# A two-layer decoder step on one Trainium2 core: the second half's first norm in steps of one feature tile, and GpSimd in written order inside the other norms

## The chip, the core and the metric

The kernel runs on one core of a Trainium2 chip. TensorE (PE in the profile) does the matmuls, VectorE (DVE), ScalarE (ACT) and GpSimd (POOL) do the elementwise work, and SyncE (SP) issues most of the transfers. The metric is the device time of one execution in microseconds (us). Lower is better.

## The reference, cut to what matters

One inference step through two layers: layer 0 mixes tokens with stick-breaking attention (16 heads of 64), layer 1 with an RWKV-7 recurrence. After each mixer comes a squared-ReLU MLP of width 4096. There are 1024 prompt tokens and 64 sample tokens (8 sequences of 8), and the model width D is 1024. Ahead of each of the four sub-layers stands an RMS norm whose shift and scale come from a conditioning vector, one vector for the prompt and one for each sample sequence:

```
def rmsnorm(x, g):
    x32 = x.astype(jnp.float32)
    y = x32 * lax.rsqrt(jnp.mean(x32 * x32, axis=-1, keepdims=True) + NORM_EPS)
    return (y * g.astype(jnp.float32)).astype(x.dtype)

def ada_norm(x, c, g, w_ada, b_ada):
    mod = jax.nn.silu(c) @ w_ada + b_ada
    shift, scale, gate = jnp.split(mod[:, None, :], 3, axis=-1)
    return rmsnorm(x, g) * (1 + scale) + shift, gate
```

The norm of sub-layer 0 feeds the q, k and v projections, those of sub-layers 1 and 3 feed the two MLPs, and that of sub-layer 2 feeds the RWKV projections.

## The kernel before, in words

**Layout and halves.** Activations lie with features on the 128 partitions and tokens along the free dimension, so x is eight feature tiles (NT = 8). The 1088 tokens are cut into two halves. Half A is columns 0 to 575, all prompt. Half B is columns 576 to 1087: 448 prompt columns and the 64 sample columns. The program goes A, then B, through each sub-layer.

**Matmuls.** Each float32 operand is split into a high part and a low part. `dense` (line 346) makes one output tile from 8 feature tiles with three matmuls for each (lines 356 to 358: high by high, low by high, high by low), into a PSUM tile `dq`. Three `dq` buffers exist. For half A one output tile takes two column groups of 288, so 48 matmuls; for half B one group of 512, so 24. A weight tile is loaded by SP (`wst`, line 339), rounded by ACT (`wh`, line 342) and its rest taken by DVE (`wl`, line 343), three buffers deep. `dn` is the copy of a finished projection tile out of PSUM, done by ACT or DVE in turn; SP then stores it.

**A norm.** `rms` (line 258) squares each feature tile on ACT (`sq`, line 265), sums over the partitions with four small matmuls for each tile (`ssq`, line 267), takes the root on ACT (`rv`, line 271), refines it with six small DVE instructions (lines 272 to 277), and spreads the result over the partitions with four matmuls (`rb`, line 281), whose copies form R. `norm_tiles` (line 313) then makes, for each feature tile, `hf` = x times R times scale, the high part `hhi` and the low part `hlo`. The prompt columns take one DVE instruction for `hf` (line 291), one on ACT for `hhi` (line 323) and one on DVE for `hlo` (line 324). The sample columns, which only half B has, take three GpSimd instructions for `hf` (lines 295 to 297), an ACT cast (line 132, reached through `split`), and one GpSimd instruction for `hlo` (line 304). `norm_split` runs `norm_tiles` through all eight tiles; it is called for sub-layers 1 and 3, for A and for B. Only the two calls for B give work to GpSimd.

**What sets the order.** Instructions are handed to a scheduling layer, which orders each engine's queue by itself: it goes through a timeline of its own and takes what is ready there, with the order of the code as priority. Each engine then runs its queue strictly in that order. Background work is a Python generator: `behind(work, rate)` registers it, and each triple of matmuls in `dense` calls `step`, which owes `rate` steps for 512 columns; one step runs the generator to its next `yield`. `beside` is a second such line.

**The start.** The norm of half A runs first. Then the projections of half A (24 output tiles) run with `second` behind them at one step for five 512-column triples. `second` is the first norm of half B. It reads x twice through `Passing` (line 102), each time in eight loads of 128 x 512 into the shared pool `n` (6 buffers), which the `dn` copies and `sq` use too. Before the change its first step is the whole of `rms`, then come eight steps of one tile each. Then the projections of half B run with attention, and later the RWKV units and chains, behind them.

Of the kernel before, what the change touches and what calls it, by code (L numbers as in the profile page):

```python
# [106 lines left out]
class Kern:  # L107
# [149 lines left out]

    def rms(self, x, pt, tmp, ps, tag, slot, rslot=None):

        nc = self.nc  # L260
        W, w = pt.W, pt.W // 4
        q = ps.tile([128, 512], F32, tag=tag, name="ssq")
        for f in range(NT):
            sq = tmp.tile([128, W], F32, tag=slot, name="sq")
            nc.scalar.activation(sq, x[f], AF.Square)
            for g in range(4):
                nc.tensor.matmul(q[32 * g:32 * g + 32, :w], self.ones32, sq[:, w * g:w * g + w],
                                 start=f == 0, stop=f == NT - 1)
        v = tmp.tile([128, 4, w], F32, tag=slot, name="rv")
        ms, r, t, y = (v[:, i, :] for i in range(4))  # L270
        nc.scalar.activation(r, q[:, :w], AF.Sqrt, bias=self.eps, scale=1.0 / D)
        nc.vector.tensor_scalar(ms, q[:, :w], 1.0 / D, EPS, ALU.mult, ALU.add)
        nc.vector.reciprocal(y, r)
        nc.vector.tensor_mul(t, y, y)
        nc.vector.tensor_mul(t, t, ms)
        nc.vector.tensor_scalar(t, t, -0.5, 1.5, ALU.mult, ALU.add)
        nc.vector.tensor_mul(r, y, t)
        R = tmp.tile([128, W], F32, tag=rslot or slot, name="R", bufs=2 if rslot else None)
        for g in range(4):
            qb = ps.tile([128, 512], F32, tag=tag, name="rb")  # L280
            nc.tensor.matmul(qb[:, :w], self.cst[:, C_SELB + 128 * g:C_SELB + 128 * g + 128], r,
                             start=True, stop=True)
            self.copy(R[:, w * g:w * g + w], qb[:, :w])
        return R

    def modulate(self, s, f, x, R, pt, t):

# [18 lines left out]
    def norm_split(self, s, x, R, pt, pool, tmp, slot):  # L306

        parts = ([], [])
        for _ in self.norm_tiles(s, x, R, pt, pool, tmp, slot, parts):
            pass  # L310
        return parts

    def norm_tiles(self, s, x, R, pt, pool, tmp, slot, parts):
# [32 lines left out]
    def dense(self, w, mts, hi, lo, pt, ps, evac):  # L346

        nc = self.nc
        kt = len(hi)
        for m in mts:  # L350
            wh, wl = self.weight(w[m])
            for c0, n in pt.ch:
                q = ps.tile([128, 512], F32, tag="dps", name="dq")[:, :n]
                for k in range(kt):
                    h, l = hi[k][:, c0:c0 + n], lo[k][:, c0:c0 + n]
                    nc.tensor.matmul(q, wh[:, k, :], h, start=k == 0, stop=False)  # L356
                    nc.tensor.matmul(q, wh[:, k, :], l, start=False, stop=False)  # L357
                    nc.tensor.matmul(q, wl[:, k, :], h, start=False, stop=k == kt - 1)  # L358
                    self.step(n)
                evac(m, c0, n, q)  # L360
# [1203 lines left out]
    def rest(self, ctx, lp, hp, xp, tmp, PS):  # L1564
        nc, I = self.nc, self.I
        A, B = HALF
        rms = lambda x, pt: self.rms(x, pt, tmp, PS, "dps", "n", "R")
        dense = lambda w, parts, pt, evac: self.dense(w, range(NT), *parts, pt, PS, evac)
        norm = lambda s, x, R, pt: self.norm_split(s, x, R, pt, hp, tmp, "n")
        self.ready = set()  # L1570

        def aside(*works, n=AS):
            with ExitStack() as ctx:
                ps = self.psum(ctx, (("aux", n),))
                for w in works:
                    yield from w(ps)

        def second(ps):

            self.RB = self.rms(Passing(self, I["x"], B, tmp), B, tmp, ps, "aux", "n", "R")  # L1580
            yield
            self.hB = ([], [])
            yield from self.norm_tiles(0, Passing(self, I["x"], B, tmp), self.RB, B, hp, tmp, "n",
                                       self.hB)


        self.load_c(tmp)
        self.load_params()
        self.load_x(A, xp)
        x = self.x  # L1590
        R = rms(x, A)
        for _ in aside(lambda ps: self.ada_steps(0, ps, "aux", (0, 4, 1, 5, 2, 6, 3, 7)), n=BG):
            pass
        self.att_setup(self.misc)
        self.xscr = self.dram.tile([NT, 128, T], F32, name="xscr")
        h = norm(0, x, R, A)
        self.behind(aside(second), 1 / 5)
        self.qkv(*h, A, tmp, PS)
        self.until(lambda: False)
        h = self.hB  # L1600
        self.behind(self.background(), RATE)
        self.beside(itertools.chain(self.ada_steps(0, PS, "aux", range(8, 12)),
                                    *(self.ada_steps(s, PS, "aux") for s in (1, 2, 3))), 40 / 180)
        self.qkv(*h, B, tmp, PS)
        self.beside(iter(()), 0.0)
        self.until(lambda: ("o", 0) in self.ready)
        self.beside(self.ahead(("o", 0), self.s_o, I["x"], A, hp, tmp), 1)
        self.beside(iter(()), 0.0)

        x, o = self.next  # L1610
        dense(I["sb_w_o"], o, A, self.residual(0, x, A, tmp))
        self.show("x1", x, A)
        R = rms(x, A)
        self.rw_setup(lp)
        self.ffn(1, x, *norm(1, x, R, A), A, hp, tmp, PS)
        self.show("x2", x, A)
        self.spill(x, A)
        self.until(lambda: ("o", 1) in self.ready)
        self.rw_late(ctx.enter_context(self.pool(name="lq", bufs=1)))
        self.ready.add("rw")  # L1620
        R = rms(x, A)
        r = self.rw_norm(x, R, A, hp, tmp)
        self.mixer_in(0, r, hp, tmp, PS, self.ahead(("o", 1), self.s_o, I["x"], B, hp, tmp))
        self.beside(iter(()), 0.0)
        x, o = self.next
        dense(I["sb_w_o"], o, B, self.residual(0, x, B, tmp))
        RB = rms(x, B)
        self.ffn(1, x, *norm(1, x, RB, B), B, hp, tmp, PS)
        self.show("x2", x, B)
        self.spill(x, B)  # L1630
        R = rms(x, B)
        r = self.rw_norm(x, R, B, hp, tmp)
        self.rw_shift()
        self.mixer_in(1, r, hp, tmp, PS, self.ahead(("y", 0), self.s_y, self.xscr, A, hp, tmp))
        self.until(lambda: ("y", 0) in self.ready)
        self.beside(iter(()), 0.0)
        x, y = self.next
        dense(I["rw_w_o"], y, A, self.residual(2, x, A, tmp))
        self.show("x3", x, A)
        R = rms(x, A)  # L1640
        self.ffn(3, x, *norm(3, x, R, A), A, hp, tmp, PS)
        self.until(lambda: False)
        with ExitStack() as ctx:
            xp = ctx.enter_context(self.pool(name="x2", bufs=8))
            xB = self.load_tiles(self.xscr, B, xp)
            y = ([], [])
            for _ in self.load_split(self.s_y, B, hp, tmp, y):
                pass
            dense(I["rw_w_o"], y, B, self.residual(2, xB, B, tmp))
            self.show("x3", xB, B)  # L1650
            R = rms(xB, B)
            self.behind(self.final(x, A, tmp, PS))
            self.ffn(3, xB, *norm(3, xB, R, B), B, hp, tmp, PS)
            self.until(lambda: False)
            for _ in self.final(xB, B, tmp, PS):
                pass
# [121 lines left out]
```

## Time and profile before

| | us |
|---|---|
| median of 3 runs | 3692.9 |
| lowest and highest run | 3689.04, 3694.14 |
| the profiled execution | 3692.01 |
| its span, first to last instruction | 3690.0 |
| PE busy in it | 3490.4 (95%) |
| DVE, ACT, POOL busy | 2326.5, 1604.9, 660.7 |

Rows of the timeline give start (us from the span's start), duration, engine, line, operation, output<-inputs, shapes, the count of merged instructions, and in brackets the engine's idle time before them with what ended it. Rows of the waits give the engine and operation that waited, what it waited for, total us, number of waits, longest. Rows of the windows give a stretch, its length, then each engine's busy us with its count of instructions, the granted TensorE clock as a share of full speed, the share of the DMA engines and the GB/s.

### The profile page before, as it was taken

To read this page: it belongs to the slowest core of one execution; us is meant where nothing else is said; L and a number is where in the kernel's file an instruction comes from. 1 tells how busy PE (TensorE), PEld (TensorE's weight loads), DVE (VectorE), ACT (ScalarE), POOL (GpSimd) and SP (SyncE) were. 2 spreads that over 40 slices of the span, in tenths; PEclk is the share of its full clock that TensorE was granted. 3 is DMA by queue.
4 is the path that set the end of the run, shared out by engine and by line. 5 is a ranking of instruction groups with operands and counts; after the bars stand their busy time and mean duration, and the time that the engine had idled before them with its cause. 6 is when DMAs were issued, how large, how long until landed. Compare 5 with 4: busy or idle time off the path is not lost.

```text
span 3690.0 us, 71087 instructions
## 1 busy us (share of the span) xinstructions
PE 3490.4 (95%) x26360; PEld 2777.1 (75%) x26360; DVE 2326.5 (63%) x4718; ACT 1604.9 (43%) x3342; POOL 660.7 (18%) x1180
## 2 busy tenths in 40 slices
PE   7999999899999999998899997989899999989998
PEld 5986667778888876876677775657788888868886
DVE  5366778785554556787846556557875666645444
ACT  4245566663333345634334445544433444432332
POOL 1023333320000001122212113021100111131111
PEclk8999999999999999999899997999899999999999
DMA  6466653319887785666344445556354444333232
GB/s 245 138 220 202 208 187 122 87 46 335 342 297 262 276 314 176 215 212 197 111 136 137 134 128 171 195 161 219 120 146 124 139 141 122 119 108 117 92 94 83
DMA packets 433003, 634.45 MB, mean 172 GB/s; under 512 B 144337, under 2 KB 244562, under 8 KB 432658
## 3 DMA queue, kind: packets, MB, share of 16 engines
q1 hardware_dynamic: 369394, 532.90, 44.6%
q10 hardware_dynamic: 63264, 97.02, 7.8%
q8 instruction: 209, 3.42, 0.4%
q14 instruction: 136, 1.11, 0.1%
HBM read 523.76 MB, written 106.01 MB: 171 GB/s over the span
## 4 chain that ended last, share of the span: by engine, by line
PE 45%; DVE 4%; DMA 3%; issue 2%; SPq 1%; ACT 1%; POOL 1%; ACTq 0%; DVEq 0%; POOLq 0%
PE dq L356 12%; PE dq L357 12%; PE dq L358 12%; PE qc L1327 1%; PE qc L1317 1%; PE qc L1336 1%; PE s L1144 1%; SPq L1215 1%; PE yq L1484 0%; PE bonq L1476 0%; DMA st<-s_st 0%; PE invq L1286 0%; PE lq L1082 0%; PE ssq L1432 0%; PE qc L1340 0%
## 5 line engine op out<-in xcount | busy, mean ns | idle before, releaser
L342 ACT CAST wh<-wst 128x512 fp32r<-128x512 f32 (+1 forms) x512 | 425.0, 834 | 756.6 <-PE dq L357 637.8
L356 PE MATMUL dq<-hhi,wh 128*128 128x288 f32 (+1 forms) x2112 | 710.2, 337 | 16.9 <-ACT hhi L132 16.1
L357 PE MATMUL dq<-hlo,wh 128*128 128x288 f32 (+1 forms) x2112 | 704.6, 334 | 5.0 <-DVE hlo L324 4.1
L358 PE MATMUL dq<-hhi,wl 128*128 128x288 f32 (+1 forms) x2112 | 703.6, 333 | 0.0
L343 DVE TENSOR_TENSOR wl<-wst,wh 128x512 fp32r<-128x512 f32 (+1 forms) x512 | 501.0, 979 | 274.5 <-ACT wh L342 245.5
L356 PE MATMUL dq<-uh,wh 128*128 128x288 f32 (+1 forms) x1536 | 509.6, 336 | 12.6 <-DVE x L371 5.9
L357 PE MATMUL dq<-ul,wh 128*128 128x288 f32 (+1 forms) x1536 | 508.0, 331 | 0.0
L358 PE MATMUL dq<-uh,wl 128*128 128x288 f32 (+1 forms) x1536 | 506.2, 332 | 1.9 <-DVE wl L343 1.9
L356 PEld LDWEIGHTS dq<-hhi,wh 128*128 128x128 f32 x2112 | 400.8, 190 | 67.3 <-issue 19.9
L357 PEld LDWEIGHTS dq<-hlo,wh 128*128 128x128 f32 x2112 | 400.6, 190 | 43.5 <-issue 7.3
L358 PEld LDWEIGHTS dq<-hhi,wl 128*128 128x128 f32 x2112 | 400.5, 190 | 41.9 <-issue 11.8
L371 DVE SCALAR_TENSOR_TENSOR x<-dq,mod,x 128x288 f32<-128x288 f32 (+1 forms) x432 | 245.9, 570 | 251.9 <-PE dq L358 249.6
L356 PEld LDWEIGHTS dq<-uh,wh 128*128 128x128 f32 x1536 | 289.1, 189 | 61.9 <-issue 15.0
L546 DVE TENSOR_TENSOR_SCAN prod<-prod 128x256 f32<-128x256 f32 (+5 forms) x264 | 242.1, 919 | 118.7 <-ACT prod L537 86.1
L358 PEld LDWEIGHTS dq<-uh,wl 128*128 128x128 f32 x1536 | 289.2, 189 | 32.2 <-issue 6.6
L357 PEld LDWEIGHTS dq<-ul,wh 128*128 128x128 f32 x1536 | 289.3, 189 | 27.0 <-issue 5.3
L377 POOL TENSOR_TENSOR x<-x,rs 128x64 f32<-128x64 f32 x144 | 118.4, 822 | 631.1 <-DVE rs L374 603.6
L356 PE MATMUL dq<-xhi,wh 128*128 128x288 f32 (+1 forms) x576 | 206.2, 358 | 4.4 <-ACT sg L974 2.1
L357 PE MATMUL dq<-xlo,wh 128*128 128x288 f32 (+1 forms) x576 | 199.4, 346 | 2.2 <-DVE xlo L304 1.8
L358 PE MATMUL dq<-xhi,wl 128*128 128x288 f32 (+1 forms) x576 | 197.9, 344 | 0.0
L547 DVE TENSOR_TENSOR beta<-beta,prod 128x256 f32<-128x256 f32 (+5 forms) x264 | 140.6, 536 | 29.0 <-POOL beta L592 8.8
L470 ACT CAST uh<-ut 128x288 fp32r<-128x288 f32 (+1 forms) x192 | 94.9, 495 | 127.5 <-DVE ut L468 127.1
(300 smaller groups left out, 6110.0 us busy)
## 6 DMA issues: line engine op xcount, KB each, us to landing
pagek<-cache_kT SPq DMA_DIRECT2D x128, 512.0 KB
pagev<-cache_v SPq DMA_DIRECT2D x128, 512.0 KB
adaw<-ada_w SPq DMA_DIRECT2D x192, 256.0 KB
wst<-w_up SPq DMA_DIRECT2D x96, 512.0 KB
wst<-w_down SPq DMA_DIRECT2D x192, 256.0 KB
st<-s_st SPq DMA_DIRECT2D x40, 672.0 KB
wst<-sb_w_qkv SPq DMA_DIRECT2D x48, 512.0 KB
wst<-w_up ACTq DMA_DIRECT2D x32, 512.0 KB
```

The lines of the kernel that those rows point to most:

```text
L342: nc.scalar.copy(wh, st)
L343: nc.vector.tensor_sub(wl, st, wh.bitcast(F32))
L356: nc.tensor.matmul(q, wh[:, k, :], h, start=k == 0, stop=False)
L357: nc.tensor.matmul(q, wh[:, k, :], l, start=False, stop=False)
L358: nc.tensor.matmul(q, wl[:, k, :], h, start=False, stop=k == kt - 1)
L371: nc.vector.scalar_tensor_tensor(xs, q[:, :np_], g, xs, ALU.mult, ALU.add)
L377: nc.gpsimd.tensor_add(xv, xv, t)
L470: nc.scalar.copy(a, t[:, :n])
L546: nc.vector.tensor_tensor_scan(r, r, r, 1.0 if carry is None else carry, ALU.mult, ALU.bypass)
L547: nc.vector.tensor_mul(beta[:, :w], beta[:, :w], p[:, 1:w + 1])
L1144: nc.tensor.matmul(qs[hd][:, 128 * x:128 * x + 128], BK[rows, u + x, 64 * hd:64 * hd + 128], AR[rows, :, c], start=True, stop=True)
L1215: nc.sync.dma_start(self.s_tt[m, r:r + 32, cs, 32 * blk:32 * blk + 32] .rearrange("s c t -> c s t"), lt[p:p + n])
```

## The change

`rms` becomes the generator `rms_steps`, which yields after each feature tile's square and sums and once at the end with R. Every caller but `second` still runs it through at once. `second` now goes through it step by step, so that its norm takes 17 background steps where it took 9. In `norm_split`, the loop over the tiles stands in a block in which GpSimd's instructions keep their written order: the scheduling layer may not move them against each other. The other engines are ordered as before, and `second`, which calls `norm_tiles` itself, is outside that block.

```
     def rms(self, x, pt, tmp, ps, tag, slot, rslot=None):

+        for R in self.rms_steps(x, pt, tmp, ps, tag, slot, rslot):
+            pass
+        return R
+
+    def rms_steps(self, x, pt, tmp, ps, tag, slot, rslot=None):
...
             for g in range(4):
                 nc.tensor.matmul(q[32 * g:32 * g + 32, :w], self.ones32, sq[:, w * g:w * g + w],
                                  start=f == 0, stop=f == NT - 1)
+            yield
...
-        return R
+        yield R
...
     def norm_split(self, s, x, R, pt, pool, tmp, slot):

         parts = ([], [])
-        for _ in self.norm_tiles(s, x, R, pt, pool, tmp, slot, parts):
-            pass
+        with self.tc.manual_schedule(engines={mybir.EngineType.Pool}):
+            for _ in self.norm_tiles(s, x, R, pt, pool, tmp, slot, parts):
+                pass
         return parts
...
-            self.RB = self.rms(Passing(self, I["x"], B, tmp), B, tmp, ps, "aux", "n", "R")
-            yield
+            for self.RB in self.rms_steps(Passing(self, I["x"], B, tmp), B, tmp, ps, "aux", "n", "R"):
+                yield
```

Lines of the changed kernel are 7 or 8 higher than those named above.

**PE in the second half's first norm.** `ssq` sums one square tile `sq`, `rb` spreads the root, and `dq` rows are the projections of half A. Before:

```order
L358 MATMUL dq_679<-hhi_433,wl_676 128x288
L267 MATMUL ssq_477<-sq_494,ones32_62 32x128 x4
L267 MATMUL ssq_477<-sq_502,ones32_62 32x128 x4
L267 MATMUL ssq_477<-sq_510,ones32_62 32x128 x4
L267 MATMUL ssq_477<-sq_518,ones32_62 32x128 x4
L267 MATMUL ssq_477<-sq_526,ones32_62 32x128 x4
L267 MATMUL ssq_477<-sq_534,ones32_62 32x128 x4
L281 MATMUL rb_551<-rv_542,cst_60 128x128
```

Now, at the third and fourth square:

```order
L365 MATMUL dq_629<-hlo_418,wh_591 128x288
L273 MATMUL ssq_480<-sq_563,ones32_62 32x128 x4
L366 MATMUL dq_629<-hhi_417,wl_592 128x288
L364 MATMUL dq_629<-hhi_423,wh_591 128x288
L365 MATMUL dq_629<-hlo_424,wh_591 128x288
L366 MATMUL dq_629<-hhi_423,wl_592 128x288
L364 MATMUL dq_629<-hhi_429,wh_591 128x288
L273 MATMUL ssq_480<-sq_608,ones32_62 32x128 x4
```

The last six sums stood in a row with `rb` right behind them. Now projection matmuls stand ahead of each of the six, 31, 5, 20, 12, 38 and 10 of them, and 47 more stand between the last sum and `rb`. The loads of x on SP's queue are spread among the stores of `dn` in the same way.

**GpSimd in the norm of sub-layer 3, half B.** Lines 295 to 297 make `hf`, line 304 makes `hlo`; the count at a row's end is of feature tiles. Before:

```order
L295 TENSOR_TENSOR hf<-x,R 128x64 x6
L296 TENSOR_TENSOR hf<-hf,mod_5465 128x64 x6
L297 TENSOR_TENSOR hf<-hf,mod_5465 128x64 x6
L304 TENSOR_TENSOR hlo<-hf,hhi 128x64 x4
L295 TENSOR_TENSOR hf<-x,R 128x64 x2
L304 TENSOR_TENSOR hlo<-hf,hhi 128x64 x2
L296 TENSOR_TENSOR hf<-hf,mod_5465 128x64 x2
L297 TENSOR_TENSOR hf<-hf,mod_5465 128x64 x2
L304 TENSOR_TENSOR hlo<-hf,hhi 128x64 x2
```

Now, with the buffer numbers kept, so that each `hf` number is one feature tile:

```order
L302 TENSOR_TENSOR hf_38917<-x_38501,R_38902 128x64
L303 TENSOR_TENSOR hf_38917<-hf_38917,mod3_5468 128x64
L304 TENSOR_TENSOR hf_38917<-hf_38917,mod3_5468 128x64
L311 TENSOR_TENSOR hlo_38923<-hf_38917,hhi_38922 128x64
L302 TENSOR_TENSOR hf_38928<-x_38503,R_38902 128x64
L303 TENSOR_TENSOR hf_38928<-hf_38928,mod3_5468 128x64
L304 TENSOR_TENSOR hf_38928<-hf_38928,mod3_5468 128x64
L311 TENSOR_TENSOR hlo_38934<-hf_38928,hhi_38933 128x64
```

Before, six tiles went through line 295, then six through 296, then six through 297, and the first `hlo` was the nineteenth instruction. Now it is the fourth, and each tile's `hlo` stands ahead of the next tile's first product. The norm of sub-layer 1, half B, shows the same two patterns.

**ACT in the norm of sub-layer 1, half B.** Here RWKV units of half A run in the background: `L`, `S` and `bkq` are theirs, `DMA s_st` and `s_l` are their stores, issued from ACT's queue. Before:

```order
L1161 COPY L<-s_20748 64x192
L271 ACT_TABLE_LOAD
L271 ACTIVATE rv<-ssq,eps 128x128
L1161 COPY L<-s_20770 64x192
L1161 COPY L<-s_20771 64x192
L1165 DMA s_st_9665<-S 64x576
L1161 COPY L<-s_20794 64x192
L1166 DMA s_st_9665<-S 128x576
L1176 COPY S<-bkq 128x320 x2
```

Now:

```order
L1173 DMA s_st_9668<-S 64x576
L1169 COPY L<-s_20801 64x192
L1173 DMA s_st_9668<-S 64x576
L1174 DMA s_st_9668<-S 128x576
L1184 COPY S<-bkq 128x320 x2
L1184 COPY S<-bkq 128x256 x2
L1189 DMA s_l<-L 128x576
L278 ACT_TABLE_LOAD
L278 ACTIVATE rv<-ssq,eps 128x128
```

The root `rv` stood ahead of most of a unit's copies. Now it stands behind all of them and behind the issue of the store `s_l`.

## The prediction

> **What bounds the kernel now.** I read the page first, then PE's waits, then windows and the timeline around the waits that the change touches.
>
> ```profile
> span 3690.0 us, 71087 instructions
> PE 3490.4 (95%) x26360; PEld 2777.1 (75%) x26360; DVE 2326.5 (63%) x4718; ACT 1604.9 (43%) x3342; POOL 660.7 (18%) x1180
> PE   7999999899999999998899997989899999989998
> ```
>
> PE is the bound: 95% busy, and at 80% or more in all slices but two. A stall of PE that goes is therefore time gained, unless a later stage gives it back. These waits of PE bear on the change:
>
> ```profile
> PE vq L140 <- ACT dn L132: 22.1, 4, 6.8
> PE ssq L267 <- ACT sq L265: 18.5, 10, 8.3
> PE dq L356 <- ACT hhi L132: 16.1, 2, 8.1
> PE rb L281 <- DVE rv L277: 16.0, 8, 3.8
> ```
>
> The third row is two waits of 8 us for the sample columns' cast. The windows show the three places (the second half's first norm; the norms of sub-layers 1 and 3 for half B) beside a steady stretch:
>
> ```profile
> 56.84:76.60 19.76, 10.35 (x77) 7.75 (x77) 7.17 (x15) 7.19 (x16) 5.64 (x11) 0.57 0.46 147
> 90.00:120.00 30.00, 30.00 (x229) 30.00 (x228) 10.25 (x13) 8.34 (x14) 3.11 (x5) 1.00 0.41 144
> 1776.87:1790.10 13.23, 5.45 (x12) 3.86 (x13) 10.62 (x19) 5.41 (x13) 13.15 (x28) 0.50 0.16 46
> 1790.10:1804.00 13.90, 13.90 (x62) 11.47 (x62) 11.89 (x30) 4.97 (x10) 1.81 (x6) 1.00 0.15 39
> 3298.40:3312.40 14.00, 5.46 (x12) 3.98 (x13) 10.17 (x15) 7.95 (x19) 13.74 (x31) 0.50 0.01 2
> ```
>
> At each place PE is idle for over 8 us and its granted clock drops to half. A steady 288-column matmul costs 30.00/229 = 0.131 us, a 512-column one 13.90/62 = 0.224 at full clock and 5.45/12 = 0.454 at half. GpSimd is busy nearly throughout the last two places.
>
> **Place 1, the second half's first norm.**
>
> ```profile
> 57.59 0.43 PE L267 MATMUL ssq<-sq,ones 128*32 128x128 f32 x8 [0.32 <-ACT sq L265]
> 57.72 7.93 SPq L102 DMA_DIRECT2D x<-x  x6
> 61.34 0.63 ACT L265 ACTIVATE sq<-x 128x512 f32<-128x512 f32 x1 [2.12 <-DMA x<-x]
> 62.02 0.65 PE L267 MATMUL ssq<-sq,ones 128*32 128x128 f32 x8 [4.01 <-ACT sq L265]
> 66.12 0.37 ACT L271 ACTIVATE rv<-ssq,eps 128x128 f32<-128x128 f32 x1 [0.82 <-PE ssq L267]
> 69.05 2.04 PE L281 MATMUL rb<-rv,cst 128*128 128x128 f32 x8 [3.05 <-DVE rv L277]
> 71.75 0.61 PE L356 MATMUL dq<-hhi,wh 128*128 128x288 f32 x1 [0.66 <-ACT dn L132]
> ```
>
> Six sums and the spread stand in a row in PE's queue, so PE waits for each load of x, then for the root, then for a copy that ACT could not do meanwhile. The window of 19.76 us holds 48 records of sums, 8 of the spread and 21 projections. At full clock they cost 6 x 0.43 + 1.0 (half of 2.04) + 21 x 0.131 = 6.4, so 13.4 is lost. Now 163 projections stand between these steps: 163 x 0.131 = 21 us for six loads and the root, 47 of them (6.2 us) ahead of the spread, where the root needs 2.9 (66.12 to 69.05). A load needed 3.6 us from issue to use (57.72 to 61.34), and 21/6 = 3.5 is there for each, with several under way. What moves with it: each x load now stands on SP between a store of `dn` and a weight load, and may hold that weight load until a buffer is free; three weight tiles, each good for 48 x 0.131 = 6.3 us, cover this. ACT squares between its `dn` copies and weight casts, and both reach PE sooner than before. The gaps of only 5, 10 and 12 projections are shorter than a load, so I keep 1.4 us of waits and count a gain of 12. Ends: 13.4 if no wait stays, 7 if three squares wait 2.12 as the one above. The eight tiles that follow keep their tile-by-tile order and lie beside projections, at no cost; if that cover were gone, they would cost what place 3 does.
>
> **Place 3, sub-layer 3, half B** (place 2 uses its terms).
>
> ```profile
> 71.53 0.77 POOL L295 TENSOR_TENSOR hf<-x,R 128x64 f32<-128x64 f32 x1 [13.01 <-ACT R L132]
> 73.08 0.24 ACT L132 CAST hhi<-hf 128x64 fp32r<-128x64 f32 x1 [0.26 <-POOL hf L297]
> 73.40 0.32 POOL L304 TENSOR_TENSOR hlo<-hf,hhi 128x64 fp32r<-128x64 f32 x1 [0.35 <-ACT hhi L132]
> 3298.43 4.13 DVE L291 SCALAR_TENSOR_TENSOR hf<-x,mod,R 128x448 f32<-128x448 f32 x6
> 3298.47 3.61 POOL L295 TENSOR_TENSOR hf<-x,R 128x64 f32<-128x64 f32 x6 [6.66 <-DVE R L134]
> 3302.48 2.62 DVE L324 SCALAR_TENSOR_TENSOR hlo<-hf,mod,hhi 128x448 fp32r<-128x448 f32 x4
> 3305.47 1.56 POOL L297 TENSOR_TENSOR hf<-hf,mod 128x64 f32<-128x64 f32 x6
> 3306.09 0.80 PE L356 MATMUL dq<-hhi,wh 128*128 128x512 f32 x1 [8.10 <-ACT hhi L132]
> 3306.98 2.30 POOL L304 TENSOR_TENSOR hlo<-hf,hhi 128x64 fp32r<-128x64 f32 x4
> 3312.00 1.39 POOL L304 TENSOR_TENSOR hlo<-hf,hhi 128x64 fp32r<-128x64 f32 x2 [0.19 <-ACT hhi L132]
> 3322.26 1.93 PE L281 MATMUL rb<-rv,cst 128*128 128x144 f32 x8 [3.81 <-DVE rv L277]
> ```
>
> Written order brings the first `hhi` three products and a cast after R, about 2.1 us, where it came after 7.6 (3298.47 to 3306.09). It also adds a wait: GpSimd now stands until ACT has cast, and behind it are queued the next tiles. A product costs 3.61/6 = 0.60 while DVE streams its own `hf`, 1.56/6 = 0.26 when DVE rests; an `hlo` 2.30/4 = 0.58 or 0.32; the cast's round trip 0.32 (73.08 to 73.40). So a tile takes 3 x 0.60 + 0.32 + 0.58 = 2.7 beside DVE and about 1.5 without. DVE streams for 8 x 0.69 + 8 x 0.66 = 10.8 us: four tiles, then four at 1.5 make 16.8. The one norm that already runs tile by tile took 2.2 for its first tile (71.53 to 73.72), or 17.6 for eight. I take 17.2: the last `hlo` lands at 3315.7, later than before (3313.4). Yet PE, which starts early, has by then done all but two matmuls of its first output tile, which ends at 3316.6. The root of the other half's final norm, also queued there, now comes behind the seventh cast, and 2.9 later its spread, at about 3316.4, no longer waits 3.81. PE passes that spread at 3316.6 where it passed it at 3322.26: 5.7 gained. Against it, PE works in bursts until then, so its clock may be at half for longer; 12 matmuls at half cost 12 x 0.23 = 2.8, of which I take 1.2. Gain 4.5. Ends: every tile at 2.7 and the full 2.8 gives a loss of 1.4; every tile at 1.5 gives a gain of 10.3.
>
> The Trainium skill, "SBUF — State Buffer", section "Who interferes with whom", says that a DVE instruction with two SBUF inputs blocks a GpSimd instruction that reads SBUF, as an exclusive lock. By that rule each GpSimd instruction beside DVE would take a whole DVE instruction (0.69), a tile 3.1, and the eight tiles 18.3 instead of 17.2, about 1 us less gain; the row of 0.60 decides, and it agrees in kind.
>
> **Place 2, sub-layer 1, half B.**
>
> ```profile
> 1769.47 0.37 ACT L271 ACTIVATE rv<-ssq,eps 128x128 f32<-128x128 f32 x1 [0.63 <-PE ssq L267]
> 1774.14 2.40 PE L281 MATMUL rb<-rv,cst 128*128 128x128 f32 x8 [2.20 <-DVE rv L277]
> 1775.14 0.41 ACTq L1181 DMA_DIRECT2D s_l<-L  x1
> 1784.57 1.65 PE L356 MATMUL dq<-hhi,wh 128*128 128x512 f32 x3 [8.03 <-ACT hhi L132]
> ```
>
> Here PE works on three output tiles at once, 72 matmuls. Before, 12 are done by 1790.10 and 60 x 0.224 = 13.4 more end at 1803.5. Now PE starts 2.1 after R, each tile brings nine matmuls (2.0 us at full clock), the last tile comes at 1776.9 + 17.2 = 1794.1, and some 13 left over end at 1797.0: 6.5 gained if the clock comes back early. If it comes back only 5.5 us (1784.57 to 1790.10) after the feed, 45 matmuls are done by 1799.6 and 27 more end at 1805.6, 2.1 lost. Nine matmuls a tile fill PE, so I take 4. Against it, the root `rv` on ACT now stands behind the background unit's copies and the issue of `s_l`, which ended at 1775.55: up to 6.1 later than 1769.47, nothing if the unit comes earlier by as much (its matmuls now precede most sums). I take 3.5. Net 0.5, ends -8.2 and 6.5.
>
> **Elsewhere.** The scheduling layer's order shifts in the middle of the program too, among independent instructions. I take 0; one wait like the longest `vq` wait, 6.8, either way.
>
> **Sum.** 12 + 0.5 + 4.5 = 17. The profiled execution took 3692.01, 2.0 over its span, so 3675; from the median of 3692.9 it is 3675.9, and I say 3676.
>
> **Rivals.**
>
> The clock stays at half through both feeds. For: all three windows with bursts show 0.50 to 0.57. Against: nine matmuls a tile at place 2. Place 2 then loses 2.1 + 3.5 = 5.6, place 3 gains 5.7 - 2.8 = 2.9: total 9.3, 3683.6. [...]
>
> The loads of x stay the bound of place 1: three more squares wait 4.01 each, the 12 is gone, 5 remain, 3688. For: the gaps of 5 to 12 projections. Against: 3.5 us for each load on average.
>
> The gain is given back where sampling ends:
>
> ```profile
> 1380.00:1410.00 30.00, 22.08 (x149) 11.98 (x142) 24.78 (x40) 20.35 (x37) 12.82 (x15) 0.76 0.66 242
> SPq L625 <- PE os L737: 277.3, 60, 11.0
> ```
>
> PE idles 8 of these 30 us. If the page transfers set that end, the 12 of place 1 is lost: 3688. Against: SP's issue of pages waits for PE (277.3 us in 60 waits), so an earlier PE means earlier pages.
>
> Slower: the shifted order in the middle puts more transposes `vq` right behind the last matmul of the tile that they turn, so PE stands through the copy `dn`. Four such waits cost 22.1 before, at most 6.8 each. There are 24 places; from three more on (20 us) the gain is gone, four more give 3692.9 - 17 + 27.2 = 3703. Against: in the changed order as many or more other matmuls stand between at most of the 24.
>
> **How the numbers follow.** A measurement of this kernel can tell about 0.2% (7.4 us) from no change. Forecast 0.64, clock 0.12, loads 0.08, sampling 0.07, slower 0.09. Faster: 0.60 of the forecast's 0.64 (the rest is same), 0.09 of the clock's, 0.05 of the next two's: 0.74. Same: 0.04 + 0.03 + 0.10 = 0.17. Slower 0.09. The range goes from 3664 (the three gains near their upper ends, 28.9 of 30.2) to 3690 (3 gained: place 1 at its lower end of 7 and 4 lost at the others), and leaves out the slower case and a little on both sides.
>
> **What would show it.** Right: sums of place 1 among projections with no wait over 2 us and no half clock there; first matmuls of places 2 and 3 about 2 us after R instead of 8, then waits of about 1 us at each tile of place 3, last `hlo` 17 us after R; the final norm's spread without its 3.8 wait; `rb` of place 2 up to 3.5 later. Wrong: waits for x at place 1 that add up to over 6 us, half clock over 20 us at place 2, or PE's waits between 1000 and 3200 us grown by more than 10 in sum.

## The result, and the profile after

The changed kernel takes 3660.95 us (median of 4, 3658.43 to 3664.95) against 3693.52 beside it: ratio 0.9919, 95% interval 0.9905 to 0.9934, 32.6 us less. The forecast was 3676, in a range of 3664 to 3690. The profiled execution took 3661.88. One of the eleven executions of kernel e4 below took 6494 us; it counts in no ratio.

The head of the page after the change:

```profile
span 3660.2 us, 71034 instructions
PE 3490.5 (95%) x26360; PEld 2764.7 (76%) x26360; DVE 2328.6 (64%) x4718; ACT 1601.2 (44%) x3341; POOL 669.3 (18%) x1180
PE   8999999899999998998899998998899999989998
```

PE's busy time is what it was (3490.4 before), in a span 29.8 us shorter. So the time came out of PE's waits. The groups of PE's waits that answer to those shown of before (total, times, longest):

```profile
PE vq L140 <- ACT dn L132: 24.4, 6, 7.2
PE rb L288 <- DVE rv L284: 12.5, 6, 5.4
PE dq L365 <- DVE hlo L332: 9.6, 6, 4.5
PE ssq L273 <- ACT sq L271: 9.2, 3, 7.8
PE dq L364 <- ACT hhi L132: 7.8, 5, 2.4
```

The sums' waits are halved (18.5 to 9.2), the two waits of 8 us for the sample columns' cast are gone (16.1 to 7.8), and those for `hlo` have grown from 4.1 us in three to 9.6 in six (2.1 us at place 3; the longest, 4.5 us at 2633.67, is at the next norm of half A).

**Place 1.** The window that was quoted of before, and PE's rows of two of its sums and of the spread behind it (squares and sums are lines 271 and 273 now, 6 higher than before):

```profile
56.84:76.60 19.76, 19.76 (x174) 17.59 (x173) 6.45 (x12) 8.00 (x14) 1.75 (x1) 1.00 0.46 164
```

```profile
58.30 0.43 PE L273 MATMUL ssq<-sq,ones 128*32 128x128 f32 x8
72.31 0.43 PE L273 MATMUL ssq<-sq,ones 128*32 128x128 f32 x8
79.00 1.05 PE L288 MATMUL rb<-rv,cst 128*128 128x128 f32 x8
```

No row has a wait, PE is full, and the clock is whole.

**Place 3.** GpSimd's first tile, its last `hlo`, and PE's first matmul and the other half's final spread:

```profile
3274.66 0.32 POOL L302 TENSOR_TENSOR hf<-x,R 128x64 f32<-128x64 f32 x1 [6.29 <-DVE R L134]
3275.06 0.56 POOL L303 TENSOR_TENSOR hf<-hf,mod 128x64 f32<-128x64 f32 x1
3276.58 0.80 PE L364 MATMUL dq<-hhi,wh 128*128 128x512 f32 x1 [2.39 <-ACT hhi L132]
3276.61 0.32 POOL L311 TENSOR_TENSOR hlo<-hf,hhi 128x64 fp32r<-128x64 f32 x1 [0.35 <-ACT hhi L132]
3279.21 0.32 POOL L311 TENSOR_TENSOR hlo<-hf,hhi 128x64 fp32r<-128x64 f32 x1 [0.35 <-ACT hhi L132]
3279.49 0.77 PE L365 MATMUL dq<-hlo,wh 128*128 128x512 f32 x1 [2.11 <-DVE hlo L332]
3292.32 0.32 POOL L311 TENSOR_TENSOR hlo<-hf,hhi 128x64 fp32r<-128x64 f32 x1 [0.35 <-ACT hhi L132]
3293.97 1.62 PE L288 MATMUL rb<-rv,cst 128*128 128x144 f32 x8 [0.54 <-DVE rv L284]
```

PE starts 2.4 us after its spread instead of 8.1. One tile takes 3279.21 - 3276.61 = 2.60 us while DVE works, the last `hlo` lands 18.0 us after GpSimd's first product (3274.66 to 3292.64), and the final norm's spread waits 0.54 us where it waited 3.81.

**Place 2.** ACT's root, PE's spread and the first `dq`:

```profile
1774.58 0.33 ACTq L1189 DMA_DIRECT2D s_l<-L  x1
1777.05 0.37 ACT L278 ACTIVATE rv<-ssq,eps 128x128 f32<-128x128 f32 x1
1779.89 2.08 PE L288 MATMUL rb<-rv,cst 128*128 128x128 f32 x8 [5.45 <-DVE rv L284]
1784.30 1.65 PE L364 MATMUL dq<-hhi,wh 128*128 128x512 f32 x3 [2.33 <-ACT hhi L132]
```

The root comes behind the store's issue, and the spread waits 5.45 us for it, 2.20 before. The feed starts after 2.3 us, not 8.0.

So places 1 and 3 did what was forecast, and place 2 in the main. To see where the rest came from, I set the two traces of PE beside each other, the k-th matmul of one against the k-th of the other. From before to after, the difference is -13.5 us at the 700th matmul (place 1 is over), -10.0 at the 6800th (900 us), -3.6 at the 11600th (1450 us), +5.4 when the spread of place 2 ends, -23.4 when that of place 3 starts and -29.8 at the end of PE's last matmul. The middle, which the forecast put at 0, lost 19 us and then gained 29:

```profile
1776.54:3295.95 1519.41, 1433.49 (x11074) 1143.46 (x11073) 978.81 (x2321) 638.37 (x1497) 244.51 (x380) 0.95 0.47 144
```

```profile
1781.97:3272.51 1490.54, 1430.09 (x11072) 1135.33 (x11073) 980.90 (x2318) 635.82 (x1496) 246.52 (x380) 0.97 0.48 146
```

These are the windows from the end of place 2's spread to the start of place 3's, before and after the change: the same 11073 matmuls, in 1519.4 and in 1490.5 us. The edited lines have only the feed of place 2 in this stretch.

### The profile page after: what moved, and what is told of

It reads as the page before. It is cut to its first block, busy times and chain, and to the rows that moved or that the text cites. A ratio compares the mean times of both kernels' runs of the same rounds, so it can differ in the third digit from the quotient of the medians.

```text
span 3660.2 us, 71034 instructions
## 1 busy us (share of the span) xinstructions
PE 3490.5 (95%) x26360; PEld 2764.7 (76%) x26360; DVE 2328.6 (64%) x4718; ACT 1601.2 (44%) x3341; POOL 669.3 (18%) x1180
## 4 chain that ended last, share of the span: by engine, by line
PE 44%; DVE 5%; DMA 3%; issue 1%; POOL 1%; ACT 1%; SPq 1%; ACTq 0%; DVEq 0%; POOLq 0%
PE dq L364 12%; PE dq L365 12%; PE dq L366 12%; PE qc L1335 1%; PE qc L1325 1%; PE qc L1344 1%; DMA s_v<-vt 1%; PE yq L1492 1%; DMA st<-s_st 0%; DVE lxn L1218 0%; PE qc L1339 0%; DVE wl L351 0%; DVE tm L1216 0%; PE s L1152 0%; PE qc L1348 0%
```

## The experiments

Three theories of the middle were tested. A: the scheduling layer, which plans with computed times, orders independent instructions anew after any edit, and the order itself is worth that much. B: written order in half B's norm of sub-layer 1 lets the later stages start earlier. C: the earlier first norm does.

All times are medians of 4 to 11 runs beside runs of the kernel before on the same chip (medians 3692 to 3694). The columns: time and ratio; how much earlier (-) or later PE is than before at the 700th, 6800th and 11600th matmul and at the end of place 2's spread; the middle (as in the two windows above); the rest, from the start of place 3's spread to the end of PE's last matmul. The last six are read from one profiled execution each. Matmuls that an edit adds are counted along, which makes these kernels look up to 1 us earlier in the three columns behind them.

| kernel | us | ratio (95%) | 700th | 6800th | 11600th | place 2 | middle | rest |
|---|---|---|---|---|---|---|---|---|
| before | 3693 | 1 | 0 | 0 | 0 | 0 | 1519.4 | 385.2 |
| changed | 3661.0 | 0.9919 (0.9905-0.9934) | -13.5 | -10.0 | -3.6 | +5.4 | 1490.5 | 378.8 |
| e7 changed again | 3660.2 | 0.9908 (0.9893-0.9923) | -13.0 | -10.5 | -5.5 | +1.3 | 1490.9 | 379.4 |
| e1 steps only | 3671.1 | 0.9951 (0.9937-0.9965) | -12.9 | -11.8 | -7.0 | -0.7 | 1500.9 | 383.6 |
| e2 GpSimd only | 3690.1 | 0.9997 (0.9987-1.0008) | +0.6 | -2.0 | +0.1 | -0.3 | 1523.3 | 378.6 |
| e3 changed, not in sub-layer 3 | 3661.0 | 0.9920 (0.9907-0.9934) | -11.3 | -10.7 | -7.3 | +0.2 | 1488.1 | 385.5 |
| e11 steps, and sub-layer 3 | 3669.1 | 0.9942 (0.9928-0.9955) | -10.5 | -9.0 | -5.6 | +4.0 | 1496.8 | 380.8 |
| e4 before, unrelated edit | 3694.7 | 1.0001 (0.9992-1.0010) | -0.8 | +2.6 | +3.4 | +12.8 | 1511.2 | 385.1 |
| e5 changed, unrelated edit | 3667.2 | 0.9922 (0.9908-0.9935) | -12.5 | -9.6 | -5.8 | -3.0 | 1501.6 | 381.5 |
| e6 changed, another one | 3691.5 | 0.9993 (0.9984-1.0002) | -12.6 | -12.4 | -12.7 | -2.7 | 1525.8 | 379.5 |
| e8 before, the changed order in the middle | 3664.2 | 0.9921 (0.9907-0.9934) | +2.4 | +1.7 | +1.6 | +5.1 | 1489.4 | 384.1 |
| e9 changed, another order in the middle | 3680.7 | 0.9964 (0.9951-0.9978) | -13.8 | -12.5 | -9.1 | +0.3 | 1513.6 | 379.5 |
| e10 changed, two unrelated edits | 3651.5 | 0.9890 (0.9875-0.9905) | -14.4 | -14.5 | -14.7 | -3.5 | 1478.4 | 379.9 |
| e12 before, the same two | 3674.7 | 0.9953 (0.9937-0.9969) | 0.0 | +0.2 | +1.7 | +18.2 | 1482.0 | 385.7 |

**The parts by themselves (e1, e2, e3).** In e1 `norm_split` is that of before. In e2 `second` is that of before. In e3:

```
-        with self.tc.manual_schedule(engines={mybir.EngineType.Pool}):
+        keep = (self.tc.manual_schedule(engines={mybir.EngineType.Pool}) if s in (1,)   # e3; e11: s in (3,)
+                else contextlib.nullcontext())
+        with keep:
```

> This kernel has only the first part of the change: half B's first norm goes one tile per step, GpSimd is ordered by the scheduling layer everywhere, as before. The changed kernel took 32.6 us less than the kernel before, and lining up the two traces of PE by their matmuls shows where: 13.5 at place 1 (between 45 and 100 us), 12 lost again by 1500, 3 to 4 more lost up to the end of place 2, then about 25 gained between 2000 and 3260, where the forecast had 0, and 5.7 at place 3. Theory A (the order that the scheduling layer gives to independent instructions in the middle is drawn anew by any edit, and the 25 is such a draw): place 1 keeps its 13.5, 8 to 12 of it are lost again by 1500, place 2 and place 3 are as before with waits of about 8 us each, and the stretch from 2000 to 3260 comes out anywhere within 15 us of before, so 3675 to 3705. Theory B (GpSimd in written order in half B's norm of sub-layer 1 is what makes the later stages shorter, since the second mixer starts with its inputs earlier): the same to 1800, and nothing gained between 2000 and 3260, so 3690 within 4. Theory C (the gain of place 1 itself reaches the middle, since the loads and casts behind it all run 13 us earlier): the 25 is gained here too, so 3665 to 3670.

> This kernel has only the second part of the change: GpSimd in written order in the other norms, half B's first norm steps as before. Up to 1700 us its order on PE is that of the kernel before, so place 1 keeps its waits and nothing differs there. Theory A (a draw of the order in the middle): place 3 gains about 5.7, place 2 is within 5 us of before, and the stretch from 2000 to 3260 comes out anywhere within 15 us of before: 3670 to 3705. Theory B (written order in the norm of sub-layer 1 shortens the later stages): the 25 us between 2000 and 3260 are gained here too, with the 5.7 of place 3: 3663 to 3668. Theory C (it comes from place 1): only the 5.7, so 3688 within 4.

> This is the changed kernel with GpSimd's order left to the scheduling layer in the norm of sub-layer 3 alone; before place 3 its instructions stand in the changed kernel's order on PE and GpSimd. By the trace of the changed kernel, place 3 was worth 5.7 us (5.4 by the end of the feed and the rest by the final norm's spread), so all theories give 3661 plus 5.7, 3666.7 within 2, if what is gained at place 3 is not given back in the 370 us behind it; it can't be, if PE is full there (3661 then would say that another bound takes over). The traces should agree within 0.5 us up to 3262 us; by how much they don't tells how far one execution's times in the middle can be trusted.

e2 speaks against B: with written order in both norms the middle is 1523, longer than before; only a worse order could hide a gain there. e1 gains 18 in the middle with the steps alone, which leaves A and C; its 3671.1 lies between the ranges that I had given for the two. The two parts don't add: beside their own runs of before, 3671 is 21 lower and 3690 is 2, together they give 32.6. e3 missed: 3661.0 instead of 3666.7, although its trace has the wait at place 3 back (385.5 against 378.8 from there on). By the start of place 3 its one profiled execution was 7.6 us ahead of the changed kernel's first and 4 ahead of its second (e7), in the same order on PE: so far may executions differ.

**Unrelated edits (e4, e5, e6, e7).** One norm's spread is issued twice; the second matmul writes the same numbers. The four more matmuls lengthen the spread by 0.6 to 1.7 us in the traces (I had said 1 us or less), and they move the computed times of what follows. `n_rms` counts the norms in the order of the program: 1 is half B's first, 2 half A's of sub-layer 1, 4 half B's of sub-layer 1.

```
-            nc.tensor.matmul(qb[:, :w], self.cst[:, ...], r, start=True, stop=True)
+            for _ in range(2 if self.n_rms == 1 else 1):     # e6: n_rms == 2; e9: 4; e8: 3 times at 4
+                nc.tensor.matmul(qb[:, :w], self.cst[:, ...], r, start=True, stop=True)
```

> The kernel before, with one edit that has nothing to do with the change: each of the four matmuls that spread the root in half B's first norm is issued twice (the second writes the same numbers again), four more matmuls of 0.25 us or less, 1 us in all. It shifts what the scheduling layer computes by that much, and the order on PE comes out different from 3000 us worth of rows on, in the middle of the program above all; places 1 to 3 stay as in the kernel before. Theory A (the middle's order is drawn anew by any edit, and this moves the time by several us): the stretch from 1780 to 3260 differs from before by more than 6 us one way or the other; the whole anywhere from 3672 to 3708, and the single-part kernels' 3671 (7 beyond the 13.5 of place 1) is such a draw. Theory C (the middle gains since the first norm's steps are spread, in whatever order): 3693 within 4, and the middle within 6 us of before.

> The changed kernel with the same unrelated edit (the spread of half B's first norm issued twice, at most 1 us). Places 1 to 3 stay as in the changed kernel. Theory A: the order in the middle is drawn anew, so most of the 25 us between 1780 and 3260 may go: anywhere from 3655 to 3690, with the sum of PE's idle time there away from the changed kernel's by more than 6 us. Theory C, or B: the gain of the middle belongs to the change, 3662 within 4.

> The changed kernel with the unrelated edit in another place: the spread of half A's norm at 740 us issued twice. A second draw of the middle. Theory A: again anywhere from 3655 to 3690, and not the same as the first draw. Theories B and C: 3662 within 4.

> The changed kernel itself once more, beside the unrelated edits on the same chip, with a second profile. Its time should be 3661 within 3. The second profile tells how far two executions of one program differ in the middle (by the kernel without written order in the norm of sub-layer 3, which has the same order on PE up to there, they differ by up to 8 us at 3260), and whether the changed kernel is really no faster than that one.

e6 speaks against C: place 1 keeps its 12.6 us (and keeps it longer than in the changed kernel, to 1450 us), place 3 keeps its gain, and four matmuls more at 740 us bring the whole back to 3691.5, since the middle takes 1525.8 us. e4 shows the other loss: without any part of the change it is 12.8 us late at place 2, as the changed kernel loses 14 to 19 between the 700th matmul and there. e5 lies between. e7 repeats the changed kernel's time and middle.

**The order alone (e8, e9).** In e8 place 2's spread is issued three times, in e9 twice. By that alone the scheduling layer gives e8, which has no part of the change, nearly the changed kernel's order on PE in the middle; e9 loses it.

> The kernel before, without any part of the change; the four matmuls that spread the root in half B's norm of sub-layer 1 (place 2) are issued three times each, eight matmuls more, 2 us at most. With this the scheduling layer happens to give PE, from 1990 us on, the order that the changed kernel has there but for four short pieces (up to 2650 us), and from there to place 3 word for word. Theory A (the gain of the middle lies in the order itself): the stretch between the spreads of places 2 and 3 takes about 1490 us as in the changed kernel, not 1519 as before; places 1 and 3 keep their waits; 3693 + 2 - 25 = 3670, 3664 to 3678. Theories B and C (the middle gains since something of the change makes its inputs come earlier): 3693 to 3697.

> The changed kernel, with the four matmuls of place 2's spread issued twice (1 us). Up to place 2 all its instructions stand as in the changed kernel, and from 2500 us on PE's order is that of the second unrelated edit, which took 3691. Theory A: the middle takes about 1520 us instead of 1490, so 3685 to 3692, though places 1 and 3 keep what they gain. Theories B and C: 3661 to 3664.

e8 takes 3664.2 us: 28.6 us are gained without the change, with places 1 and 3 as slow as before. e9 loses 20; its middle takes 1513.6 where I had said 1520, and its 3680.7 us are below the 3685 to 3692 that I had given. The windows of the middle in e8, and in e6 for the other end:

```profile
1781.68:3271.10 1489.42, 1425.82 (x11073) 1132.98 (x11073) 978.01 (x2321) 634.66 (x1496) 243.89 (x380) 0.97 0.49 146
```

```profile
1773.84:3299.62 1525.78, 1442.18 (x11073) 1150.37 (x11073) 982.41 (x2322) 637.49 (x1497) 245.56 (x380) 0.95 0.48 143
```

Again the same 11073 matmuls, in 1489 and 1526 us: PE idles 63.6 and 83.6, and its clock is 0.97 and 0.95. e8 settles A, since its middle gains without any part of the change, which B and C both need: the order is worth up to 36 us here.

What such an order costs can be seen where before and e8, alike up to place 2, part most. The windows of before, then of e8, from place 2 to the second mixer and over half A's last MLP:

```profile
1780.00:2300.00 520.00, 492.79 (x3524) 374.31 (x3525) 318.44 (x755) 224.71 (x540) 113.77 (x201) 0.95 0.45 136
2660.00:2860.00 200.00, 183.00 (x1531) 166.79 (x1530) 133.97 (x331) 71.22 (x169) 9.01 (x18) 0.94 0.50 139
```

```profile
1785.00:2310.00 525.00, 507.03 (x3725) 378.23 (x3727) 318.65 (x778) 231.16 (x574) 112.58 (x204) 0.96 0.46 138
2660.00:2860.00 200.00, 196.81 (x1690) 181.72 (x1689) 130.32 (x323) 76.44 (x190) 11.29 (x19) 0.98 0.45 131
```

PE's idle time falls from 27.2 to 18.0 us in the first and from 17.0 to 3.2 in the second, and e8 runs 201 and 159 matmuls more in them. In the second, before, PE waits for weight casts and residual sums; one such place, on DVE, ACT and PE:

```profile
2690.76 0.91 DVE L1203 MEMSET lxn<- 128x1024 f32 x1 [5.20 <-DMA s_tt<-llt]
2692.41 0.62 ACT L342 CAST wh<-wst 128x512 fp32r<-128x512 f32 x1 [12.46 <-DVE lxn L1204]
2693.17 0.37 PE L356 MATMUL dq<-uh,wh 128*128 128x288 f32 x1 [2.77 <-ACT wh L342]
2695.55 0.61 PE L358 MATMUL dq<-uh,wl 128*128 128x288 f32 x1 [1.88 <-DVE wl L343]
```

A background unit's memset heads DVE's queue and waits 5.2 us, by the profile for a store of the unit before. Behind it stand the residual sums and `wl`; ACT's cast of the next weight comes after it too (the profile ends its 12.46 us of waiting with the small memset that follows, line 1204), and PE stands. In e8 the same memset runs earlier, at the start of this MLP, and PE has no wait between 2635 and 2650 us:

```profile
2641.53 0.91 DVE L1205 MEMSET lxn<- 128x1024 f32 x1 [1.75 <-issue]
```

**The change at a nearly equal order (e10, e12), and place 3 again (e11).** e10 is the changed kernel with place 2's spread issued four times and that of half A's norm at 740 us twice; e12 is the kernel before with the same. PE's order is then nearly the same in both: by the lines and tiles of the two traces it differs at the three places (behind place 2 up to 1887 us of e12), in one piece at 1376 to 1424 us, where sampling ends, and in four matmuls at 2780 us.

```
+            for _ in range({2: 2, 4: 4}.get(self.n_rms, 1)):
```

> The changed kernel with place 2's spread issued four times and that of half A's norm at 740 us twice (16 matmuls more, 3 us at most). The second unrelated edit reached the spread of place 2 some 4 to 8 us earlier than the changed kernel (1773.8 against 1782.0 and 1777.9); behind it this kernel has the order of the changed kernel from 2050 us on but for the same short pieces. Theory A: the good order ahead of place 2 and the good one behind it, 3661 + 3 - 6 = 3658, 3648 to 3664. If the early lead is only chance of an execution: 3660 to 3666.

> The kernel before, without any part of the change, with the same two unrelated edits as the last but one kernel (place 2's spread issued four times, that of half A's norm at 740 us twice). With these, PE's order is the same with and without the change but at places 1, 2 and 3 themselves and two short pieces at 1540 and 1620 us, so this kernel against that one (3651.5) prices the change at equal order. Theory A, with the forecast's terms (place 1 13.5, place 2 about 0, place 3 5): 3651.5 + 18.5 = 3670, 3666 to 3674, and the stretch between the spreads of places 2 and 3 within 6 us of 1478. If the change reaches the middle in some other way than by its order (theories B and C): above 3676, and a longer middle.

> The first part of the change with GpSimd in written order in the norm of sub-layer 3 alone. Up to place 3 (3260 us) PE and GpSimd have the order of the kernel with the steps alone, which took 3671.1. This asks once more in time for the gain of place 3, which the traces give as 5.4 to 6.1 us and the times of the kernel without it (3661.0 against 3661.0 and 3660.2) do not show: 3665 within 2 if the trace is right, 3671 if something gives it back that the trace of PE does not show.

e10 takes 3651.5 us (3641.95 to 3654.25), less than both kernels, with 16 matmuls too many. e12 takes 3674.7, just above my 3666 to 3674, so the change is worth 23 us at a nearly equal order (the ratios differ by 0.0063, with an uncertainty of 0.0022, or 8 us): the forecast's 17 lies inside. The heads of the two pages:

```profile
span 3640.2 us, 71097 instructions
PE 3478.7 (96%) x26392; PEld 2761.4 (76%) x26392; DVE 2324.1 (64%) x4718; ACT 1602.6 (44%) x3341; POOL 673.2 (18%) x1180
```

```profile
span 3671.2 us, 71109 instructions
PE 3489.5 (95%) x26392; PEld 2773.3 (76%) x26392; DVE 2326.2 (63%) x4718; ACT 1601.9 (44%) x3341; POOL 670.0 (18%) x1180
```

Matmul by matmul, e12 falls behind e10 by 14.4 us at place 1, stands at 14.7 at the 11000th, loses 7 between 1370 and 1710 us, 3 in the feed of place 2, next to nothing over the next 10000 matmuls (25.1 at their start, 25.3 at their end), and 5.7 at place 3. Of the 7, 1.8 lie in the piece whose order differs; the rest lies in the same order, and the profile of e10 is of its fastest run, 3641.95.

e11 against e1, and e3 against the changed kernel, ask for place 3 in times: 2.0 and 0 us. The traces say 5.1: from place 3's spread to the end eight executions with written order take 378.6 to 381.5 us, six without 383.6 to 385.7. Single runs of one kernel spread over 6 to 17 us, so medians of five can't price 5. That the trace is right is likely from 14 executions, and the times have not confirmed it.

## Why the prediction was wrong

**Place 1: right.** Forecast 12 of 13.4, measured 13.5 and 13.0 in two executions (10.5 to 14.4 over all nine with the steps). The 1.4 us of waits that I kept did not come. The rival in which the loads of x stay the bound is out: no sum waits.

**Place 3: right, by its mechanism and size.** Forecast a gain of 4.5; 72 matmuls after the spread end 32.7 us behind it where they ended 38.1 behind it, 5.4 less. A tile beside DVE takes 2.60 (forecast 2.7, with luck in its terms: `hlo` took 0.32 there, not 0.58, and the waits between the products make up for part of it), the last `hlo` comes at 18.0 (17.2), and the final spread's 3.8 us of waiting shrank to 0.5. The clock was at half for 10.2 us, where it had been for 17.1 and once more for 3.4, so the rival that the feed stays cold fails in this execution. It does not fail in all: over the eight executions with written order here the clock was at half for 10.2 to 20.5 us, and in that of e11 (20.5) the 72 matmuls end at 34.5, a gain of 3.6, near that rival's 2.9. The upper end of 10.3 does not follow from the terms shown: eight tiles at 1.5 end 5.2 before 17.2, which makes 9.7 with the 4.5. The rule of the Trainium skill, "SBUF — State Buffer", section "Who interferes with whom", would have made a tile 3.1 us. A tile's three products took 0.70, 0.56 and 0.56 and its `hlo` 0.32, so not each a whole DVE instruction, and the row was the better guide.

**Place 2: right in sum, off in its terms.** The root's delay was sized at 3.5 and cost 5.45 - 2.20 = 3.25. The feed was sized at a gain of 4; the 72 matmuls end 26.0 us behind the spread instead of 27.5, so 1.4. The clock stayed at half for 23.9 us, 27.3 before: here the rival was nearly right, and over 20 us at half was one of the signs that I had named for being wrong (27.3 again in the second execution). Net a loss of 1.9, inside the ends given.

**Elsewhere: this step failed.** "I take 0; one wait like the longest `vq` wait, 6.8, either way." The order of the middle was not a matter of one wait. PE lost 14 to 19 us between place 1 and place 2's spread (3.25 of them the root's) and gained 29 from there to place 3, and edits to one norm's spread put that second stretch anywhere from 1489 to 1526 us. I had seen that the order shifts, and priced it by the worst single wait of a kind that I could name. Its price had to be read from a spread of orders: kernels without the change come out at 3664 to 3695, kernels with it at 3651 to 3692, on the same three places.

**Given back at the end of sampling: seen in part, but not by its cause.** The changed kernel does lose 6.5 us between the 11050th and the 11600th matmul. Its longest wait there, and after it that of e6:

```profile
1377.58 0.61 PE L364 MATMUL dq<-xhi,wh 128*128 128x288 f32 x1 [5.58 <-ACT xhi L132]
```

```profile
1374.11 0.69 PE L140 MATMUL tq<-cst,beta 128*128 128x128 f32 x2 [5.50 <-DVE beta L557]
```

Page transfers that set the end would do so in e6 as well, which comes there 2 us earlier still and loses nothing (-12.4 to -12.7). So the transfers do not set that end. Waiting alone does not explain the loss either: in this stretch PE idles 12.9 us before, 17.6 in the changed kernel and 17.0 in e6, while the clock is at half for 17.1, 23.9 and 10.2 us. Four executions with the changed kernel's order there (changed, e3, e7, e9) lose 3.5 to 6.6 us at 17.1 to 23.9 us of half clock. Why the clock comes back sooner in e6 is open.

**Slower through `vq`: no.** Those waits went from 22.1 to 24.4 us.

So of the 32.6 us some 16 (13.2 + 5.1 - 1.9 by the traces) to 23 (by e10 against e12) belong to the change, and the rest is the order that it happened to bring. What stays open: which of the waits in the middle make up how much of the 29 us (the two windows give 25 us of idle time), and where the rest of the loss between 1450 and 1780 us lies, since two executions of the changed kernel differ by 4 us at its end.

## What to carry to other kernels

Where a scheduling layer orders the queues by computed times, an edit can also draw a new order for the rest of the program, and a forecast needs a term for that draw, as wide as a few unrelated edits make it. Price an edit against a twin that has the same order elsewhere, or over several unrelated edits, before its time is put down to it. A wait at the head of an in-order queue (here a memset that waits for a store) costs what stands behind it, so look at what the queue's next instructions feed.

## What the runs showed of the hardware

- One program's executions are not one timeline: the changed kernel's two profiled executions end place 2's spread at 1782.0 and 1777.9 us, and the four runs of e10 go from 3641.95 to 3654.25 us.
- At place 3 of the changed kernel a GpSimd product of 128x64 takes 0.55 to 0.70 us while DVE runs its own `hf` and `hlo` (0.32 the first, which starts 0.04 us behind DVE's), and 0.29 to 0.32 when DVE rests. `hlo`, which starts as the cast ends, takes 0.32 in both.
- At place 3 of the changed kernel the granted clock was at half for 10.2 us and then stayed whole, although PE had waited 2.39 and 2.11 us inside that time and waits 0.64 and 0.57 us behind it. The same feed had 10.2 to 20.5 us of half clock over eight executions.
- About the same idle time goes with very different clocks: between the 11050th and the 11600th matmul PE idles 17.6 us with 23.9 us at half clock in the changed kernel, and 17.0 us with 10.2 us at half in e6.
